# A hybrid encoder layer: the front in another order, keys loaded ahead, W steps and gathers placed elsewhere

## The chip, the cores and the metric

The kernel runs on one core of a Trainium2 chip. The metric is device time in microseconds of one execution. TensorE (PE in the rows) multiplies, VectorE (DVE), ScalarE (ACT) and GpSimd (POOL) do the rest; SyncE (SP), ScalarE and GpSimd issue the transfers.

## The reference

One layer over 528 tokens (16 meta tokens and 512 of the sequence) of width 1024, cut to what matters:

```python
xn = rmsnorm(h, ln1_w)
dq, dk, dv, gq, gk, gv, gr, zf, zb = split(xn @ w_in)
da = rmsnorm(diff_attention(rope(dq), rope(dk), dv, lam, pos), da_subln_w) * (1 - lam_init)   # 4 heads
go = rmsnorm(gla_bidirectional(gq, gk, gv, log_g_f, log_g_b), gla_norm_w) * silu(gr)          # 4 heads
h = (h + concat(da, go) @ w_out)[16:]
# product keys: 8 heads, 2 x 128 keys, 16 of each, 16 of the 256 sums; 128 experts a token
q = rmsnorm(h, ln2_w) @ w_q                       # 512 x (8, 2, 128)
ts, ti = top_k(q @ sub_keys, 16)                  # per head and half
best, pos = top_k(ts[0][:, None] + ts[1], 16)     # idx of 16384 experts, gate = softmax(best)
out = h + sum_k (gate * gelu(hn . u[idx])) * v[idx]
return rmsnorm(out, final_norm_w)
```

## The kernel before, in words

Every product in float32 is made of three: both operands are split into a `hi` and a `lo` half (`hi` cast by ScalarE at L118, `lo = raw - hi` by VectorE or POOL at L120), and L131 to L133 multiply hi by hi, lo by hi and hi by lo.

The **front** (0 to about 365 us) follows the string `ORDER`, a letter a step: `G` and `g` draw the next part of the two generators of GLA (one for each pair of heads), `x` is the projections of the second pair, `v`, `k` and `q` the projections of attention (`q` ends with a rotation of the positions and a product with the meta keys at L471), `u` one of 16 attention units (L490, L491 the scores, L515, L516 transposes, L522 the values), `w` one of eight output products over the GLA half. The weights are streamed in the order of the same string. At the end of a GLA head its output is transposed at L769.

Then come the second half of the output products, the second norm (L893 its sums, L903 its factors as a row by a product of `ones` and the diagonal tile `dg`), 16 **query products** and behind each the scores against the keys (L953). VectorE picks 16 of 128 per token, head and half (`top16`, L188 to L192), then 16 of the sums (`topk2`, L196 to L255: candidates, positions, expert numbers and the softmax, whose result is written to `sel` at L255); L992 computes the expert numbers `idx` of the first 128 tokens.

The experts are used in two ways. For 384 of the 512 tokens all 16384 experts are computed densely, in 128 **u tiles** (24 matmuls of 128 x 384 each, gelu at L1094) and 128 **v tiles**, weighted by a matrix W that TensorE builds from one-hot vectors: 48 **W steps** of 8 tokens, each with transposes of `sel` first where a new 128 tokens begin (L1002), one-hot operands `oh` from VectorE (L1024, L1029), 32 small matmuls (L1060, L1063) and an evacuation (L1065). The dense results of the first `LA` = 60 u tiles are spilled to memory and so is W, and come back with the v tiles. For the other 128 tokens rows of u and v are **gathered** by indirect DMAs that POOL issues (L264), 128 of each; VectorE dots the u rows (L278) and adds up the v rows (L276).

The numbers that set the mix: W step n stands behind u tile `A0 + int(n * AR)`, and 10 later from step 14 on, where the last two `topk2` stand between; `GS0` is the u tile from which on gathers are issued, `RA` the gathers per u tile from there on, `RV` those per v tile up to the 60th and `RUV` behind it. `lo` of u tiles 0 to 13 is made on POOL, from 14 on on VectorE (`LP` = 14). Within these anchors a scheduler orders the instructions of every engine; tiles with a common tag share buffers, so that a load waits for the last reader of what lay there.

Of the kernel before, what the change touches and what calls it, by code (L numbers as in the profile page):

```python
# [9 lines left out]
F32 = mybir.dt.float32  # L10
# [14 lines left out]
P = 128  # L25
# [9 lines left out]
PH = 8  # L35
NK = 128
# [6 lines left out]
AHEAD = 2  # L43
LAG = 3
GP = 0
GS0 = 12
C1 = 3.0
WB = 4
WL = 1
# [10 lines left out]
VS = 4  # L60
VR = 5
VG = 6
RA = 0.3
RV = 0.85
RUV = 2.92
LA = 60
NCAND = 80
TCA = {'schedule_with_timeline_sim': True}
ORDER = 'GGGxGGGGGGGkGGggvgqggukugguqugguuukuvgqgukqgwuwuuuwwwuuuww'
ATAG = 'a'  # L70
BTAG = '-p'
BL = 32
# [5 lines left out]
PF = 3, 13, 2  # L78
PG = 33, 49, 1
LP = 14  # L80
A0 = 15
AR = 0.48
AG = 10
AL = 14

# [1 line left out]
def _emit(ctx, tc, I, out):  # L87
    nc = tc.nc
# [48 lines left out]
    def split(hi, lo, src, eng=None):  # L137
        last[0] = nc.scalar.copy(hi, src).ins.name  # L138
        (eng or nc.vector).tensor_sub(lo, src, hi.bitcast(F32))  # L139
# [40 lines left out]
    def tz(name, shape, dt=F32):  # L180
        tag = "t" + TMAP[name]
        return f2.tile(list(shape), dt, name=name, tag=tag, bufs=TBUF[TMAP[name]])

    def fx(name, shape, tag, dt=F32):
        return f1.tile(list(shape), dt, name=name, tag=tag)
# [113 lines left out]
    cnt = dict.fromkeys("vkqgGxuw", 0)  # L299
    for step in ORDER + "w" * (KD - ORDER.count("w")):  # L300
        n = cnt[step]
# [506 lines left out]
    cnt = dict.fromkeys("vkqgGxuw", 0)  # L808
    for step in ORDER:
        n = cnt[step]  # L810
# [59 lines left out]
    def hn_hi(k):  # L870
        return hg[k // 4][0][:, k % 4, :]

    def hn_lo(k):
        return hg[k // 4][1][:, k % 4, :]
# [21 lines left out]
    nc.scalar.copy(hss, hs[:, :NT])  # L896
    rstd(hrs, hss, D)
    nc.vector.scalar_tensor_tensor(hn0, acc0, hrs[:, 0:1], hn0, op0=ALU.mult, op1=ALU.mult)
    dg = tz("dg", [P, 4, P])
    for t in range(NT):  # L900
        nc.vector.tensor_scalar(dg[:, t, :], ident, hrs[:, t:t + 1], None, op0=ALU.mult)
    b = bank(tag=PT["nat"])
# [16 lines left out]
    qs = qst.enter_context(tc.tile_pool(name="qs", bufs=1))  # L919

    iof = w1.tile([P, NK], F32, name="iof")
    nc.sync.dma_start(out=iof, in_=I["iota"].to_broadcast([P, NK]))
    keys = qs.tile([P, 2 * PH, NK], F32, name="keys")
    nc.sync.dma_start(out=keys, in_=I["keys"])

    tsv = tk1.tile([P, 2, NT, 4, 2, TOPK], F32, name="tsv")
    tiv = tk1.tile([P, 2, NT, 4, 2, TOPK], U32, name="tiv")
# [11 lines left out]
    for k in range(KD):  # L939
        hk = qs.tile([P, ND], F32, name="hk", bufs=2)  # L940
        nc.gpsimd.tensor_add(hk, hn_hi(k)[:, P:].bitcast(F32), hn_lo(k)[:, P:].bitcast(F32))
        nc.gpsimd.tensor_mul(hk, hk, hrow[:, P:])
        split(un_hi[:, k, :], un_lo[:, k, :], hk, nc.gpsimd)

    tks = []
    for hp in range(2 * PH):
# [34 lines left out]
    def wbuild():  # L981
        def tgt(n):
            return A0 + int(n * AR) + (AG if n >= AL else 0)

        def fin_all(at):
            while fins:
                fins.pop(0)(at)

        for tk in tks:
            for _ in tk:  # L990
                pass
        nc.vector.scalar_tensor_tensor(idx, sel[:, 1, 0].rearrange("p h r -> p (h r)"), float(NK),  # L992
                                       sel[:, 2, 0].rearrange("p h r -> p (h r)"), op0=ALU.mult, op1=ALU.add)
        yield A0 - 2
        fin_all(A0 - 2)
        cur = {}
# [132 lines left out]
    def pull(n):  # L1129
        credit[0] += n  # L1130
        while credit[0] >= 1.0:
            credit[0] -= 1.0
            next(sp, None)
# [12 lines left out]
    def w_load(b):  # L1146
        if b * WI < NK and b not in WA:
            wa = vp.tile([P, 2, WI, ND], F32, name="wa", bufs=3)
            wt = wa[:, 0].rearrange("p w n -> p (w n)").rearrange("p (b w n) -> p b w n", w=WI, n=BL)
            nc.sync.dma_start(out=wt, in_=W_d[:, :, b * WI:b * WI + WI, :])  # L1150
            if b * WI < LA:
                nc.sync.dma_start(out=wa[:, 1], in_=A_d[:, b * WI:b * WI + WI, :])
            WA[b] = wt, wa[:, 1]
# [5 lines left out]
    for i in range(LA):  # L1159
# [4 lines left out]
        if i == LA - ET:  # L1164
# [5 lines left out]
            w_load(0)  # L1170
        if GS0 <= i < LA - ET - GP:
            pull(RA)

    acts = {}
    for i in range(NK):
# [12 lines left out]
        if i >= VS:  # L1188
            pull(RV if i < LA else RUV)
    for _ in sp:  # L1190
# [112 lines left out]
```

## Time and profile before

| | before |
|---|---|
| median of 3 runs | 1642.83 us (1638.16 to 1642.96) |
| profiled execution | 1635.18 us |
| its span, first to last instruction | 1633.4 us |
| TensorE busy | 1561.7 us (96%) |
| VectorE busy | 1261.5 us (77%) |
| mean granted clock of TensorE | 0.985 |

The rows below are of the one profiled execution; what lies around its span is 1.8 us. A busy share of TensorE contains its stretches at the lower clock.

### The profile page before, as it was taken

The page shows a single profiled execution, that of the slowest core. Times are in us where ns is not written, and L with a number is a line of the kernel's source. Part 1 is how long each engine was busy: PE and PEld are TensorE (multiplying, and loading weights), DVE is VectorE, ACT ScalarE, POOL GpSimd, SP SyncE. Part 2 cuts the span into 40 slices and gives each one's busy share as a digit, 9 for nine tenths or more (in the row PEclk, how much of TensorE's full clock was granted, in tenths as well). Part 3 has the DMA queues.
Part 4 walks back from the last instruction along what each step waited for, and adds up shares of the span by engine and source line. Part 5 has one row for each costly group of instructions (what it writes and reads, how often), then busy time and mean ns, then how long its engine had stood idle before and what let it go on. Part 6 is the DMA issues. An engine that isn't in the chain of part 4 may idle for free.

```text
span 1633.4 us, 24035 instructions
## 1 busy us (share of the span) xinstructions
PE 1561.7 (96%) x8793; PEld 1382.3 (85%) x8793; DVE 1261.5 (77%) x2492; ACT 712.7 (44%) x1131; POOL 563.7 (35%) x419
## 2 busy tenths in 40 slices
PE   6999999999997789999999999999999999999997
PEld 6887886778897788989888888889999999998886
DVE  3888767655999796977467787788878887787877
ACT  5444654544332466777343333333333333333333
POOL 3445113048553330040011112265454443444442
PEclk9999999999999899999999999999999999999999
DMA  7112212233233466778999998799999999999975
GB/s 235 59 48 83 66 55 69 84 104 118 79 133 112 133 235 241 296 265 304 375 350 323 319 315 312 272 369 360 324 348 330 330 338 318 329 353 328 331 252 193
DMA packets 152358, 387.40 MB, mean 237 GB/s; under 512 B 12752, under 2 KB 71376, under 8 KB 150576
## 3 DMA queue, kind: packets, MB, share of 16 engines
q1 hardware_dynamic: 104432, 213.62, 38.0%
q0 software_dynamic: 36864, 134.23, 23.2%
q10 hardware_dynamic: 10944, 38.02, 6.2%
q8 instruction: 69, 1.13, 0.3%
q14 instruction: 49, 0.40, 0.1%
HBM read 342.56 MB, written 40.63 MB: 235 GB/s over the span
## 4 chain that ended last, share of the span: by engine, by line
PE 46%; issue 19%; DVE 15%; DMA 10%; POOL 7%; ACT 2%; SPq 1%; POOLq 0%; ACTq 0%; DVEq 0%
POOL gat L264 7%; PE bankg L131 6%; PE bankg L133 6%; PE bankg L132 6%; PE banka L1119 5%; PE banka L1122 5%; PE banka L1123 5%; DMA gat<-v,idx 4%; DMA gat<-u,idx 3%; PE bankp L1123 2%; PE bankp L1122 2%; PE bankp L1119 2%; DVE tiv L192 1%; DVE tiv L189 1%; DVE sc L190 1%
## 5 line engine op out<-in xcount | busy, mean ns | idle before, releaser
L264 POOL DMA_INDIRECT gat<-u,idx x128 | 201.6, 1575 | 531.2 <-PE bankp L1123 251.6
L118 ACT CAST hi<-raw 128x1024 fp32r<-128x1024 f32 x177 | 185.8, 1051 | 320.3 <-PE bankg L132 191.1
L131 PE MATMUL bankg<-un_hi,hi 128*128 128x384 f32 x896 | 303.4, 339 | 3.9 <-ACT act L1094 3.9
L132 PE MATMUL bankg<-un_lo,hi 128*128 128x384 f32 x896 | 302.5, 338 | 0.0
L133 PE MATMUL bankg<-un_hi,lo 128*128 128x384 f32 x896 | 302.3, 338 | 0.0
L264 POOL DMA_INDIRECT gat<-v,idx x128 | 157.7, 1232 | 206.7 <-PE bankp L1123 172.7
L120 DVE TENSOR_TENSOR lo<-raw,hi 128x1024 fp32r<-128x1024 f32 x142 | 174.0, 1227 | 56.3 <-ACT hi L118 52.4
L276 DVE SCALAR_TENSOR_TENSOR acc<-gat,sact,acc 128x1024 f32<-128x1024 f32 x128 | 164.3, 1284 | 58.1 <-DMA gat<-v,idx 55.0
L278 DVE CUSTOM_DVE_ANT_0 gat<-gat,hn 128x1024 f32<-128x1024 f32 x128 | 155.1, 1219 | 36.8 <-DMA gat<-u,idx 36.1
L139 DVE TENSOR_TENSOR vhl<-vraw,vhl 128x1024 fp32r<-128x1024 f32 x128 | 156.1, 1220 | 27.6 <-ACT vhl L138 26.5
L131 PEld LDWEIGHTS bankg<-un_hi,hi 128*128 128x128 f32 x896 | 169.6, 189 | 7.9 <-ACT act L1094 4.2
L132 PEld LDWEIGHTS bankg<-un_lo,hi 128*128 128x128 f32 x896 | 169.5, 189 | 3.3
L133 PEld LDWEIGHTS bankg<-un_hi,lo 128*128 128x128 f32 x896 | 169.6, 189 | 1.7 <-DVE lo L120 0.2
L138 ACT CAST vhl<-vraw 128x1024 fp32r<-128x1024 f32 x128 | 134.2, 1049 | 55.8 <-PE bankp L1123 34.6
L120 POOL TENSOR_TENSOR lo<-raw,hi 128x1024 fp32r<-128x1024 f32 x35 | 87.1, 2491 | 73.7 <-ACT hi L118 70.1
L1065 ACT ACTIVATE stg<-banka 128x512 f32<-128x512 f32 x96 | 96.9, 1165 | 11.4 <-PE banka L1063 11.0
L1094 ACT ACTIVATE act<-bankg 128x384 f32<-128x384 f32 x112 | 54.5, 487 | 30.2 <-PE bankg L133 20.7
L133 PE MATMUL bankp<-un_hi,lo 128*128 128x384 f32 x128 | 44.6, 348 | 21.9 <-DVE lo L120 21.9
L1024 DVE TENSOR_TENSOR oh<-iT,ioh 128x2048 f16<-128x2048 f16 x48 | 57.5, 1219 | 1.3 <-PE banka L1063 1.3
L1029 DVE TENSOR_TENSOR oh<-oh,gs 128x2048 f16<-128x2048 f16 x48 | 57.7, 1218 | 0.0
L1060 PE MATMUL banka<-oh 128*128 128x128 f16 x384 | 49.5, 221 | 8.2 <-DVE oh L1029 7.3
L1063 PE MATMUL banka<-oh 128*128 128x128 f16 x384 | 49.1, 220 | 0.0
(2287 smaller groups left out, 3775.1 us busy)
## 6 DMA issues: line engine op xcount, KB each, us to landing
raw<-uT SPq DMA_DIRECT2D x128, 512.0 KB
vraw<-v SPq DMA_DIRECT2D x128, 512.0 KB
W_d<-stg ACTq DMA_DIRECT2D x12, 2048.0 KB
wa<-W_d SPq DMA_DIRECT2D x32, 768.0 KB
A_d<-act ACTq DMA_DIRECT2D x60, 192.0 KB
wa<-A_d SPq DMA_DIRECT2D x15, 768.0 KB
raw<-wq SPq DMA_DIRECT2D x16, 512.0 KB
raw<-win_n SPq DMA_DIRECT2D x12, 512.0 KB
```

The costliest lines, as they stand in the source:

```text
L118: nc.scalar.copy(hi, raw)
L120: (eng or nc.vector).tensor_sub(lo, raw, hi.bitcast(F32))
L131: nc.tensor.matmul(o, lhsT=ah, rhs=bh, start=start, stop=False)
L132: nc.tensor.matmul(o, lhsT=ah, rhs=bl, start=False, stop=False)
L133: return nc.tensor.matmul(o, lhsT=al, rhs=bh, start=False, stop=stop)
L138: last[0] = nc.scalar.copy(hi, src).ins.name
L139: (eng or nc.vector).tensor_sub(lo, src, hi.bitcast(F32))
L264: g = nc.gpsimd.indirect_dma_start(out=r, out_offset=None, in_=src, in_offset=bass.IndirectOffsetOnAxis(ap=idx[:, hk:hk + 1], axis=0))
L276: nc.vector.scalar_tensor_tensor(acc0, r, sact[:, hk:hk + 1], acc0, op0=ALU.mult, op1=ALU.add)
L278: nc.vector.tensor_tensor_reduce(r, r, hn0, scale=1.0, scalar=0.0, op0=ALU.mult, op1=ALU.add, accum_out=sact[:, hk:hk + 1])
L1119: m0 = nc.tensor.matmul(o, lhsT=gh_[:, tc_], rhs=vh[:, dc], start=(j == 0), stop=False, skip_group_check=True)
L1122: nc.tensor.matmul(o, lhsT=gh_[:, tc_], rhs=vl[:, dc], start=False, stop=False, skip_group_check=True)
```

## The change

Five numbers and the string are others, the keys' load is issued behind the loop that makes `un_hi`, in the program's order, and the diagonal tile lies in another place:

```diff
-GS0 = 12
+GS0 = 20
...
-RA = 0.3
+RA = 0.15
 RV = 0.85
-RUV = 2.92
+RUV = 3.0
...
-ORDER = 'GGGxGGGGGGGkGGggvgqggukugguqugguuukuvgqgukqgwuwuuuwwwuuuww'
+ORDER = 'GGxGGvGkGGGqGGGGggugkugguqguguvgkuguqgugkuguqwuwuwuwuwuwuww'
...
-A0 = 15
-AR = 0.48
+A0 = 11
+AR = 0.56
...
-    dg = tz("dg", [P, 4, P])
+    dg = fx("dgh", [P, 4, P], "gvs")
...
     iof = w1.tile([P, NK], F32, name="iof")
     nc.sync.dma_start(out=iof, in_=I["iota"].to_broadcast([P, NK]))
-    keys = qs.tile([P, 2 * PH, NK], F32, name="keys")
-    nc.sync.dma_start(out=keys, in_=I["keys"])
...
         split(un_hi[:, k, :], un_lo[:, k, :], hk, nc.gpsimd)
+    keys = qs.tile([P, 2 * PH, NK], F32, name="keys")
+    nc.sync.dma_start(out=keys, in_=I["keys"])
```

The first W steps stand behind u tiles 11 to 18 (before 15 to 21), the others behind 28 to 47 (before 31 to 47).

What that does to the engines' order. SP's queue at the keys, as a piece of the difference (`raw<-wq` are blocks of the query weights, `hT_d` parts of the layer's input written out):

```order
 L112 DMA raw<-wq 128x1024
 L853 DMA hT_d<-hT_3443 128x384
 L853 DMA hT_d<-hT_3460 128x384
 L112 DMA raw<-wq 128x1024
+L943 DMA keys<-keys 128x2048
 L922 DMA iof<-iota 128x128
-L924 DMA keys<-keys 128x2048
 L112 DMA raw<-wq 128x1024 x11
```

The keys stand one row ahead of `iof` instead of behind it.

TensorE at the end of the front, before (`mix` are the output products of a `w` step, `rdst` the rotated queries of head 3, whose product with the meta keys is L471):

```order
L133 MATMUL bankg<-mix_hi_2963,lo 128x512
L131 MATMUL bankg<-mix_hi_2963,hi 128x512
L132 MATMUL bankg<-mix_lo_2965,hi 128x512
L133 MATMUL bankg<-mix_hi_2963,lo 128x512
L132 MATMUL bankg<-mix_lo_2965,hi 128x512
L133 MATMUL bankg<-mix_hi_2963,lo 128x512
L471 MATMUL bankp<-rdst,kb 32x512
L515 MATMUL banka<-ident,pr 128x128 x4
L516 MATMUL banka<-ident,pr 32x128
L769 MATMUL banka<-ident,gy 128x128
L490 MATMUL banka<-stl,stq_2685 128x512
L491 MATMUL banka<-stk_2404,stq_2685 128x512
```

and in the change (`stq_2982` and `stq_2983` are the queries of head 3):

```order
L515 MATMUL bankp<-ident,pr 128x128 x4
L516 MATMUL bankp<-ident,pr 32x128
L490 MATMUL banka<-stl,stq_2982 128x512
L490 MATMUL banka<-stl,stq_2983 128x512
L515 MATMUL banka<-ident,pr 128x128 x4
L516 MATMUL banka<-ident,pr 32x128
L522 MATMUL bankp<-vN_494,aT 128x128
L522 MATMUL bankp<-vN_495,aT 128x128
L522 MATMUL bankp<-vN_496,aT 128x128
L522 MATMUL bankp<-vN_497,aT 128x128
L522 MATMUL bankp<-vN_498,aTm 128x128
L471 MATMUL bankp<-rdst,kb 32x512
```

L471 of head 3 stood right behind an output product and ahead of the last GLA head's transposes. It now stands behind attention units of head 2, behind the first two score products of head 3, and behind all of L769.

TensorE at the first score product L953, before (the query products of the weights' columns, `hg` being the normed input):

```order
L132 MATMUL banka<-hg_lo_3504,hi 128x512
L133 MATMUL banka<-hg_hi_3503,lo 128x512
L131 MATMUL banka<-hg_hi_3647,hi 128x512
L132 MATMUL banka<-hg_lo_3648,hi 128x512
L133 MATMUL banka<-hg_hi_3647,lo 128x512
L131 MATMUL banka<-hg_hi_3647,hi 128x512
L953 MATMUL bankg<-keys,pq 128x128 x4
L132 MATMUL banka<-hg_lo_3648,hi 128x512
```

and in the change, from L903 on, with the row ahead of it:

```order
L133 MATMUL bankg<-hg_hi_3647,lo 128x512
L903 MATMUL banka<-dgh,ones 128x512
L131 MATMUL banka<-hg_hi_3503,hi 128x512
L132 MATMUL banka<-hg_lo_3504,hi 128x512
L131 MATMUL banka<-hg_hi_3503,hi 128x512
L132 MATMUL banka<-hg_lo_3504,hi 128x512
L953 MATMUL bankg<-keys,pq 128x128 x4
L133 MATMUL banka<-hg_hi_3503,lo 128x512
```

Before, 40 query matmuls stand between L903 and the first L953, in the change 4. The number of query matmuls behind L903 is the same, 312.

VectorE where the top-k of the first 256 tokens ends, before, from the expert numbers L992 to the second write of the gates (L255):

```order
L992 SCALAR_TENSOR_TENSOR idx<-sel 128x128
L220 TENSOR_SCALAR sm_row<-sm_bp 128x128
L221 TENSOR_SCALAR sm_bp<-sm_bp 128x128
L226 CAST sm_rf<-sm_row 128x128
L227 CAST sm_cf<-sm_bp 128x128
L229 SCALAR_TENSOR_TENSOR sm_t_6141<-sm_rf,sm_cf 128x128
L120 TENSOR_TENSOR lo<-raw,hi 128x1024 x3
L253 TENSOR_REDUCE zs<-sm_gate 128x8 x2
L254 RECIPROCAL zs<-zs 128x8 x2
L255 TENSOR_TENSOR sel<-sm_gate,zs 128x2x64 x2
L210 TENSOR_TENSOR sm_gate<-sm_bsv 128x128
L278 ISA gat,sact<-gat,hn_70 128x1024
```

and in the change, from the last write of the gates on:

```order
L255 TENSOR_TENSOR sel<-sm_gate,zs 128x2x64
L220 TENSOR_SCALAR sm_row<-sm_bp 128x128
L210 TENSOR_TENSOR sm_gate<-sm_bsv 128x128
L247 TENSOR_TENSOR sel<-eq 128x2x64
L210 TENSOR_TENSOR sm_gate<-sm_bsv 128x128
L221 TENSOR_SCALAR sm_bp<-sm_bp 128x128
L226 CAST sm_rf<-sm_row 128x128
L212 TENSOR_TENSOR sm_gate<-sm_gate,hrs 128x128
L239 TENSOR_TENSOR eq<-sm_cb,io16b 128x2048
L212 TENSOR_TENSOR sm_gate<-sm_gate,hrs 128x128
L227 CAST sm_cf<-sm_bp 128x128
L120 TENSOR_TENSOR lo<-raw,hi 128x1024
```

The gates' two writes are no longer behind three `lo` of u tiles but in among the last steps of the top-k: ahead of the second one stand L239, L243, three rows of L245 and L253 to L255 that were behind `idx`. The first `lo` that VectorE makes (u tile 14's) stands 11 rows behind it. On TensorE, the transposes of `sel` (L1002) stand behind 308 matmuls of u tiles, before behind 384, and the first matmul of a W step behind 399, before 473; the 14 tiles whose `lo` POOL makes are 336.

## Rows read from the trace of the kernel before

**Rows 1.** The page: the span, and the busy us, share of the span and instructions of each engine.

```profile
span 1633.4 us, 24035 instructions
...
PE 1561.7 (96%) x8793; PEld 1382.3 (85%) x8793; DVE 1261.5 (77%) x2492; ACT 712.7 (44%) x1131; POOL 563.7 (35%) x419
```

**Rows 2.** The waits of TensorE over the whole span: line and operand waited for, us in total, times, longest.

```profile
PE bankp L133 <- DVE lo L120: 21.9, 2, 19.7
...
PE banka L1060 <- DVE oh L1029: 7.3, 5, 3.4
...
PE bankg L131 <- ACT act L1094: 3.9, 1, 3.9
PE bankg L582 <- POOL hi L577: 3.2, 1, 3.2
```

**Rows 3.** Stretches of 30 us: length, then busy us and instructions of each engine, the granted clock of TensorE, the share of DMA and its GB/s.

```profile
270.00:300.00 30.00, 26.00 (x95) 16.60 (x93) 21.05 (x53) 15.59 (x50) 4.14 (x3) 0.77 0.20 56
510.00:540.00 30.00, 10.25 (x59) 9.93 (x58) 29.93 (x174) 2.87 (x4) 1.46 (x2) 0.75 0.09 31
570.00:600.00 30.00, 24.86 (x192) 23.64 (x189) 28.35 (x33) 17.33 (x21) 1.48 (x2) 0.94 0.57 202
600.00:630.00 30.00, 26.59 (x207) 25.45 (x206) 25.90 (x27) 18.68 (x23) 13.78 (x2) 0.94 0.75 278
1500.00:1530.00 30.00, 29.34 (x148) 26.29 (x148) 23.91 (x25) 10.23 (x14) 11.51 (x11) 1.00 0.92 335
```

**Rows 4.** The timeline of TensorE at the end of the front: start, us, engine, line, operation, output and inputs, shapes, count, and in brackets the idle time before it with what ended it.

```profile
260.43 0.40 PE L133 MATMUL bankg<-act_hi,lo 128*128 128x512 f32 x1
...
273.02 1.02 PE L471 MATMUL bankp<-rdst,kb 128*32 128x512 f32 x2 [1.98 <-DVE ss L144]
...
276.79 0.30 PE L769 MATMUL banka<-ident,gy 128*128 128x128 f32 x1 [1.89 <-DVE gy L765]
...
290.34 0.63 PE L132 MATMUL bankg<-mix_lo,hi 128*128 128x512 f32 x1
...
292.87 0.39 PE L132 MATMUL bankg<-mix_lo,hi 128*128 128x512 f32 x1
293.10 0.39 PE L133 MATMUL bankg<-mix_hi,lo 128*128 128x512 f32 x1
```

**Rows 5.** The timeline where the query products begin, of TensorE, SyncE's DMA queue (SPq) and VectorE.

```profile
364.62 0.95 PE L893 MATMUL banka<-ones,sq 128*128 128x1 f32 x8
...
373.04 1.02 PE L903 MATMUL banka<-dg,ones 128*128 128x512 f32 x2
...
374.13 0.33 SPq L922 DMA_DIRECT2D iof<-iota  x1
374.55 0.38 SPq L924 DMA_DIRECT2D keys<-keys  x1
...
383.01 1.05 PE L953 MATMUL bankg<-keys,pq 128*128 128x128 f32 x8
...
385.84 0.87 DVE L188 MAX8 tsv<-sc 128x8 f32<-128x128 f32 x4 [16.78 <-issue]
...
393.29 0.88 DVE L188 MAX8 tsv<-sc 128x8 f32<-128x128 f32 x4 [2.67 <-ACT sc L955]
```

**Rows 6.** The timeline of VectorE and TensorE around the long wait.

```profile
519.39 0.34 PE L132 MATMUL bankp<-un_lo,hi 128*128 128x384 f32 x1
...
520.31 1.21 DVE L243 TENSOR_TENSOR eq<-eq,tf 128x2048 bf16<-128x2048 bf16 x1
...
536.96 0.27 DVE L992 SCALAR_TENSOR_TENSOR idx<-sel 128x128 int32<-128x128 f32 x1
...
539.47 0.69 PE L133 MATMUL bankp<-un_hi,lo 128*128 128x384 f32 x1 [19.75 <-DVE lo L120]
...
548.04 0.49 DVE L255 TENSOR_TENSOR sel<-sm_gate,zs 128x128 f32<-128x128 f32 x2
```

**Rows 7.** The timeline of POOL, VectorE and TensorE from 555 to 620 us.

```profile
555.22 12.05 POOL L264 DMA_INDIRECT gat<-u,idx  x1 [15.91 <-PE bankg L133]
...
570.39 1.23 DVE L278 CUSTOM_DVE_ANT_0 gat<-gat,hn 128x1024 f32<-128x1024 f32 x1 [3.94 <-DMA gat<-u,idx]
...
573.95 0.44 PE L133 MATMUL bankp<-un_hi,lo 128*128 128x384 f32 x1 [2.16 <-DVE lo L120]
...
585.38 0.44 PE L131 MATMUL bankp<-un_hi,hi 128*128 128x384 f32 x1 [2.98 <-ACT hi L118]
...
616.13 1.23 DVE L278 CUSTOM_DVE_ANT_0 gat<-gat,hn 128x1024 f32<-128x1024 f32 x1 [4.10 <-DMA gat<-u,idx]
...
619.69 0.23 PE L1060 MATMUL banka<-oh 128*128 128x128 f16 x1 [3.41 <-DVE oh L1029]
```

**Rows 8.** The page's costliest groups: line, engine, operation, output and inputs, count, then busy us, mean ns of one, and the idle time before them with what ended most of it.

```profile
L264 POOL DMA_INDIRECT gat<-u,idx x128 | 201.6, 1575 | 531.2 <-PE bankp L1123 251.6
...
L1024 DVE TENSOR_TENSOR oh<-iT,ioh 128x2048 f16<-128x2048 f16 x48 | 57.5, 1219 | 1.3 <-PE banka L1063 1.3
```

**Rows 9.** The timeline of POOL and TensorE at the end.

```profile
1605.16 0.94 POOL L264 DMA_INDIRECT gat<-v,idx  x1 [0.30 <-issue]
1606.40 1.05 POOL L264 DMA_INDIRECT gat<-v,idx  x1 [0.30 <-issue]
...
1625.44 0.39 PE L1123 MATMUL bankp<-vhl,gl__15068 128*128 128x512 f32 x1
```

## The prediction

> **What bounds the kernel now.** I read the busy shares first [rows 1]: TensorE works 1561.7 of 1633.4 us and VectorE 77%, so only what stops TensorE or slows its clock moves the end, and there are 71.7 us without a matmul. The waits of TensorE [rows 2] say on what: 21.9 on `lo` of u tiles, one wait alone 19.7; 7.3 on `oh`, the one-hot operands of the W steps; 3.9 on `act` at the change to the v tiles; and waits of 3.2 or less in the front. The stretches of 30 us [rows 3] add what waits don't show: the granted clock is 0.77 in 270 to 300, 0.75 around the long wait and 0.94 in the two stretches from 570 to 630, while VectorE is full (29.93 of 30) ahead of 540. Late in the v tiles TensorE has 29.34 of 30 us with DMA at 0.92. So three places matter: the end of the front, the hole at 520 to 540 with what follows until 630, and the last microseconds.
>
> **The front's last part.** In the kernel before, the query gemm of head 3 ends near 260.7, its product with the meta keys (L471) starts at 273.02 after a wait of 1.98, and the last GLA head's transposes (L769) then wait 1.89 at 276.79 [rows 4]. The same output product that takes 0.39 at 292.87 takes 0.63 at 290.34: half clock, 1.2 instead of 2.4 GHz. At a mean of 0.77 over 30 us this costs at most (1 - 0.77) x 30 = 6.9 [rows 3]. So the place holds 3.9 us of waits and up to 6.9 of slow clock. In the order of the change the GLA step is drawn ahead of query gemm 3, its transposes stand amid attention and output products, and L471 comes later: between the gemm and the first product that needs its rope stand 24 output products, at 0.23 each by their spacing at 292.87 [rows 4] 5.5 us, and 12 score products and some 30 small products, which I estimate at another 8: 13.5. The chain took 273.02 - 260.7 = 12.3. Both waits should go: -3.9. Whether the clock then stays up I can't read; I take half, -3: **-7**, bounds -10.8 (all of it) and +6 (a stretch of the new front waits for its gates or its rope and falls to half clock as this one did). The earlier part of the front keeps its work and gets projections between the GLA levels instead of behind them; I put it at 0.
>
> A rule of the Trainium skill speaks against counting on this ("TensorE: Matmul & The Clock Gate", section HAM oscillation): the slow clock is the default state, and a stretch in which TensorE idles enough throws it back, once for each such stretch. The trace agrees in that the clock is low at the short waits of the front as well as at the hole [rows 3]. By the rule each wait of the new order may bring a slow stretch of its own, the front's term is -3.9 instead of -7, and the sum below 3 us higher.
>
> **Keys.** Before, the load of `keys` stands behind `iof` on SP's queue; `iof` is issued at 374.13, when L903 (373.04) has freed the buffer it needs, and `keys` follows at 374.55. The first score product L953 starts at 383.01 and the first top-k operation at 385.84, after VectorE had idled 16.78 [rows 5]. In the change `keys` stands ahead of `iof` and waits only for L893 (364.62, 0.95 long): issue at about 365.6, 9 earlier. It took 383.01 - 374.55 = 8.5 to be used, so 374.1 is the earliest; TensorE's order has L953 four matmuls behind L903, 373.04 + 0.9 + 4 x 0.23 = 374.9. The top-k starts 385.84 - 383.01 = 2.8 later, as before: 377.7, **8.1 earlier**. Not all of it arrives: a head-part costs VectorE 393.29 - 2.67 - 385.84 = 4.8 us, and now 17 to 30 query matmuls (4 to 7 us) stand between score groups, so it starves until second-level work is at hand. Before it starved 2.67 there; I take 4 (2.7 to 7).
>
> **The hole.** The top-k work up to `idx` (L992, 536.96) is 536.96 - 385.84 - 2.67 = 148.4 us [rows 5, 6]. In the change it ends at 377.7 + 148.4 + 4 = 530.1. Ahead of the second gate write (L255), on which the transposes L1002 wait, now also stand L239 and L243 (1.21 each [rows 6], both on 128x2048), three L245 on half, a quarter and an eighth of that (about 1.2) and L253 to L255 (about 1.3, the last pair being 0.49): 5. So `sel` is there at 535.5. TensorE comes to L1002 28 matmuls sooner than it came to the missing `lo` (539.47 - 19.75 = 519.7); a u matmul of 384 columns, priced from the 512 columns of [rows 4], is 0.23 x 384 / 512 = 0.17: 519.7 - 4.8 = 514.9. Hole 20.6 instead of 19.75: the 28 matmuls given up eat what the keys bring. **+1**, bounds -4 (top-k fed without a gap) and +8 (first rival). The half clock behind the hole stays.
>
> **Behind the hole.** From 555 to 620 TensorE waits 2.16 for a `lo`, 2.98 for a `hi` and 3.41 for an `oh` [rows 7], and the clock's 0.94 in two stretches costs (1 - 0.94) x 60 = 3.6 [rows 3]: 12 us. The first and the third stand behind 3.94 and 4.10 in which VectorE sat before a gathered row (L278); the gather's issue on POOL ahead of the first had taken 12.05 us, against a mean of 1.575 [rows 7, 8]. With gathers from u tile 20 on and half as many per tile, VectorE's order has its first L278 behind the W steps of the first batch: no such wait, and four dots of 1.23 fewer. Against it the 14 W steps of that batch (two VectorE operations of 1.22 each [rows 8]) begin some 75 matmuls (13 us of TensorE) sooner among the u tiles, and the `lo` of tiles 14 and 15 stand behind parts of the last top-k: tile 15's comes, by its place in VectorE's order, about 13 us behind L255, when TensorE wants it after 9.4, a new wait of 3.5. 12 - 3.5 - 2 for its clock gives **-6**, bounds -11 and +3 (VectorE, not the gathers, was the limit, and the waits return with 3.5 more). In the second batch both orders ask for about as much VectorE work per TensorE work: 0. Nor is a change seen at the 3.9 us before the v tiles: 0.
>
> **Late gathers and the tail.** At 0.15 per u tile instead of 0.3, 4.5 instead of 11.4 gathers are done by u tile 49; the rest catches up at 3.0 instead of 2.92 per tile, and three instead of two fall into the last slot. POOL is busy 11.51 of 30 us late in the v tiles [rows 3], so the added ones are hidden; the last is not. Gathers at the end come 1606.40 - 1605.16 = 1.24 apart, 19 us ahead of the last matmul at 1625.44 [rows 9], to which their sums lead through the last weights. One more costs 1.24 and what its DMA adds: **+1.5**, bounds 0 and +4. More gather bytes per tile (2.7% of them) at a DMA share of 0.92 I put at 0, since TensorE hardly waits there.
>
> **Sum.** -7 + 1 - 6 + 1.5 = -10.5. The profiled execution took 1635.18 with its span of 1633.4; the span would be 1622.9, that execution 1624.7. It lies 7.65 below the median of the runs shown (1642.83), so on their scale 1632.3: **1632 us**. A measurement of this kernel can tell about 0.3% (4.9 us) from no change.
>
> **Rivals.**
> - *The transposes wait longer* (slower). If the keys' lead is lost (the load lands late, or VectorE starves by all of it), `sel` comes at 537.2 + 5 + 0.5 = 542.7, and TensorE stands at 514.9: a hole of 27.8, +8. VectorE then is as late as before for the batch, so the -6 goes; with -3.9 in the front and +1.5 at the end +5.6: 1648. It decides where the top-k starts after 381 instead of 377.7. Against it: SP's order frees the load from L903. Chance 0.12.
> - *The new front falls to half clock itself* (the rule above): front +6, sum +2.5, 1645. For it speaks that waits of 2 us went with a slow stretch [rows 3, 4], against it the 13.5 to 12.3 at the place known. Chance 0.15, half of it within 0.3%.
> - *Only the keys and the gathers act*: the front gives 0 and the stalls half, -0.5: 1642, no change. Chance 0.12.
> - *The late gathers bound the end*: POOL falls behind by five gathers of 1.24, +6 at the tail: sum -6, 1637. Chance 0.06.
> - *Everything goes*: hole -4, stalls -11, front -10.8, tail +1.5: -24, 1619. Chance 0.08.
> - The forecast, -5 to -18 (1625 to 1638): 0.47.
>
> Faster: the forecast, everything, and half of the fourth, 0.58. Within 0.3%: the third, half of the second, half of the fourth and a little of the first: 0.24. Slower: the rest, 0.18. The range leaves out the worst hole and the deepest gain: 1617 to 1646; the forecast's own is 1625 to 1638.
>
> **What would show it.** `keys` issued about 365.6 and the first top-k operation about 378; one hole of 19 to 22 us, released by `sel` at L1002 and no longer by `lo`; no VectorE wait on a gathered row before 620; a wait of some 3 us on the `lo` of the next tiles; no waits at L471 and L769 in the front and a clock of 0.9 or more in 260 to 300; three gathers in the last slot. The prediction is wrong if the front shows a new slow stretch, if L1002 waits more than 24, or if `oh` waits grow past 8.

## The result and the profile after

| | before | change |
|---|---|---|
| median of 4 runs each | 1640.86 us (1638.16 to 1642.96) | 1659.26 us (1657.55 to 1660.74) |
| ratio, 95% interval | | 1.0113 [1.0095, 1.0132] |
| span of the profiled execution | 1633.4 us | 1658.7 us |
| mean granted clock of TensorE | 0.985 | 0.969 |

The change is 1.1% slower, where 0.6% faster was forecast. The busy shares of the changed kernel, from its page, beside [rows 1]:

```profile
span 1658.7 us, 24025 instructions
...
PE 1573.5 (95%) x8793; PEld 1391.2 (84%) x8793; DVE 1263.4 (76%) x2492; ACT 716.5 (43%) x1131; POOL 533.8 (32%) x419
```

As many matmuls as before are busy 11.8 us longer, and the time without one grew from 71.7 to 85.2. The loss is in the front. Stretches from the start to where the second norm begins (L893), first of the kernel before, then of the changed one (columns as in [rows 3]):

```profile
0.00:364.60 364.60, 340.91 (x2109) 281.12 (x2110) 255.89 (x573) 188.96 (x418) 114.07 (x112) 0.98 0.28 90
```

```profile
0.00:398.90 398.90, 356.64 (x2111) 291.58 (x2111) 254.09 (x573) 190.88 (x418) 106.11 (x112) 0.92 0.26 82
```

The front is 34.3 us longer: 18.6 of it without a matmul (23.7 to 42.3), 15.7 in the same matmuls running longer, at a clock of 0.92. From L893 to the end the changed kernel takes 1259.8 instead of 1268.8, 9 less. (The two profiled executions differ by 25.3 and the medians by 18.4: that of before lies 6 below its median.)

The waits of TensorE in the changed kernel over the whole span, beside [rows 2]:

```profile
PE bankp L1002 <- DVE sel L255: 24.5, 1, 24.5
PE banka L769 <- DVE gy L765: 9.0, 2, 8.9
...
PE bankg L131 <- ACT act L1094: 5.2, 1, 5.2
PE banka L710 <- DVE ef L706: 3.6, 1, 3.6
...
PE banka L1119 <- ACT gh__15064 L138: 2.7, 1, 2.7
```

The hole is released by `sel` now. New are 8.9 at the transposes L769 and 3.6 at L710 (transposes for the GLA's state); 2.7 at L1119, a product of the v tiles at the very end, was 1.1. Where they lie and what the clock does, in stretches of 30 us:

```profile
120.00:150.00 30.00, 18.01 (x67) 11.43 (x66) 22.32 (x60) 12.13 (x24) 8.74 (x8) 0.69 0.13 39
150.00:180.00 30.00, 27.64 (x175) 23.70 (x176) 14.86 (x39) 11.90 (x27) 8.21 (x8) 0.85 0.12 32
...
270.00:300.00 30.00, 29.04 (x104) 20.49 (x102) 14.88 (x50) 9.98 (x31) 5.34 (x5) 0.69 0.06 13
300.00:330.00 30.00, 25.52 (x107) 16.03 (x106) 22.36 (x64) 18.38 (x50) 4.17 (x3) 0.89 0.23 64
...
600.00:630.00 30.00, 29.93 (x255) 28.67 (x254) 28.69 (x29) 21.83 (x26) 0.00 (x0) 1.00 0.68 253
```

The front has two slow places, 120 to 180 and 260 to 330; behind the hole TensorE is full again soon. The first place in TensorE's timeline (L471 is the first `q`'s product with the meta keys, L619 makes the gates' logits):

```profile
122.33 1.04 PE L471 MATMUL bankp<-rdst,kb 128*32 128x512 f32 x2 [1.54 <-DVE rdst L407]
...
137.59 0.48 PE L754 MATMUL banka<-S,qx 64*128 64x128 f32 x2
137.92 0.29 PE L619 MATMUL bankp<-zT,w 64*128 64x16 f32 x2
147.06 0.45 PE L769 MATMUL banka<-ident,gy 128*128 128x128 f32 x1 [8.86 <-DVE gy L765]
...
147.87 0.79 PE L753 MATMUL banka<-S,qx 64*128 64x128 f32 x2
```

and in VectorE's, in the gap (L641 and L672 belong to the gates of the next pair of heads, L144 to L147 and L765 to the norm of the pair that is done):

```profile
139.83 1.37 DVE L641 TENSOR_TENSOR_SCAN pre<-ones,garr 128x129 f32<-128x129 f32 x4
...
141.91 0.16 DVE L144 TENSOR_SCALAR ss<-ss 128x4 f32<-128x4 f32 x1
...
143.81 0.74 DVE L641 TENSOR_TENSOR_SCAN pre<-ones,garr 128x129 f32<-128x129 f32 x2
...
146.58 1.13 DVE L765 SCALAR_TENSOR_TENSOR gy<-go,rs,gr 128x128 f32<-128x128 f32 x4
```

The norm's small steps go in turn with the next pair's gates, and TensorE's next instruction is the one that needs their end. The query projection (`q`) that could stand there was drawn four GLA steps earlier. Behind the gap the GLA products run at the slow clock: two of L753 take 0.79, where two of L754, of the same shape, took 0.48 ahead of it. The gap is not the only slow stretch there. The clock in stretches of 3 us (columns as above):

```profile
126.00:129.00 3.00, 3.00 (x7) 2.00 (x7) 2.15 (x6) 0.00 (x0) 0.21 (x1) 0.50 0.46 115
...
135.00:138.00 3.00, 3.00 (x20) 2.34 (x18) 0.38 (x2) 0.00 (x0) 0.00 (x0) 1.00 0.00 0
...
150.00:153.00 3.00, 3.00 (x11) 2.33 (x12) 0.83 (x3) 0.00 (x0) 0.00 (x0) 0.50 0.00 0
```

Half clock (1.2 GHz) comes first behind the waits of 1.5 at L471, the end of the early `q`, and 0.8 right after it, until about 131, and again from the gap to about 159.

### The profile page after: what moved, and what is told of

The parts are those of the page before. It is cut to its first block, busy times and chain, and to the rows that moved or that the text cites. A ratio compares the mean times of both kernels' runs of the same rounds, so it can differ in the third digit from the quotient of the medians.

```text
span 1658.7 us, 24025 instructions
## 1 busy us (share of the span) xinstructions
PE 1573.5 (95%) x8793; PEld 1391.2 (84%) x8793; DVE 1263.4 (76%) x2492; ACT 716.5 (43%) x1131; POOL 533.8 (32%) x419
## 4 chain that ended last, share of the span: by engine, by line
PE 66%; DVE 15%; DMA 6%; issue 6%; ACT 4%; POOL 3%; SPq 1%; ACTq 0%; POOLq 0%; DVEq 0%
PE bankg L131 9%; PE bankg L132 9%; PE bankg L133 9%; PE banka L1122 7%; PE banka L1119 7%; PE banka L1123 7%; PE bankp L1119 3%; PE bankp L1122 3%; PE bankp L1123 3%; DMA raw<-uT 1%; DVE oh L1024 1%; POOL lo L120 1%; DVE lo L120 1%; PE banka L656 1%; ACT stg L1065 1%
## 5 line engine op out<-in xcount | busy, mean ns | idle before, releaser
L264 POOL DMA_INDIRECT gat<-u,idx x128 | 169.6, 1325 | 566.9 <-PE bankp L1123 238.0
L264 POOL DMA_INDIRECT gat<-v,idx x128 | 169.2, 1322 | 181.3 <-PE bankp L1123 153.8
L1060 PE MATMUL banka<-oh 128*128 128x128 f16 x384 | 48.5, 220 | 3.0 <-DVE oh L1029 2.1
L131 PE MATMUL bankg<-act_hi,hi 128*128 128x264 f32 (+1 forms) x144 | 48.6, 337 | 1.9 <-ACT rraw L400 1.9
L131 PE MATMUL bankg<-hi,act_hi 128*128 128x256 f32 x160 | 46.4, 290 | 2.1 <-ACT vN L777 1.4
```

The costliest lines, as they stand in the source:

```text
L131: nc.tensor.matmul(o, lhsT=ah, rhs=bh, start=start, stop=False)
L264: g = nc.gpsimd.indirect_dma_start(out=r, out_offset=None, in_=src, in_offset=bass.IndirectOffsetOnAxis(ap=idx[:, hk:hk + 1], axis=0))
```

## The experiments

The theory under test first: the loss is the query projection drawn too early, which leaves TensorE nothing behind the first pair's norm, and the slow clock that follows the wait. Against it: the loss comes only with the other edits, or it lies in the later part of the order, at the place of `v` or elsewhere.

All are timed against the kernel before. "Rest" is the span less the start of L893, from the profiled execution. Kernels with the front of before (e2, e5 to e9) start L893 at 359.3 to 367.4, so one profile tells some 4 us either way there. The profiled executions lie between 6 us below and 10 us above the medians of their kernels (e1 10 above, e8 9, e12 and e14 5).

| kernel | ratio [95%] | L893 at | rest |
|---|---|---|---|
| before | 1 | 364.6 | 1268.8 |
| change | 1.0113 [1.0095, 1.0132] | 398.9 | 1259.8 |
| e1, order only | 1.0179 [1.0146, 1.0213] | 397.2 | 1281.2 |
| e2, all but the order | 0.9919 [0.9886, 0.9952] | 367.2 | 1261.5 |
| e3, change with `q` later | 1.0014 [0.9992, 1.0036] | 376.4 | 1261.5 |
| e12, e3 with `v` later | 1.0019 [0.9993, 1.0045] | 387.6 | 1260.1 |
| e4, first third of the order | 1.0086 [1.0061, 1.0111] | 376.5 | 1271.2 |
| e14, e4 with `q` later | 1.0030 [1.0002, 1.0059] | 371.5 | 1278.4 |
| e13, later part of the order | 1.0040 [1.0014, 1.0066] | 366.0 | 1273.9 |
| e10, two letters exchanged | 0.9965 [0.9940, 0.9989] | 361.9 | 1270.3 |
| e7, keys | 0.9972 [0.9950, 0.9995] | 363.4 | 1270.5 |
| e5, gathers | 0.9940 [0.9922, 0.9959] | 364.4 | 1258.1 |
| e6, W steps | 1.0086 [1.0053, 1.0120] | 359.3 | 1284.3 |
| e8, keys and W steps | 1.0031 [1.0001, 1.0061] | 364.9 | 1285.9 |
| e9, keys and gathers | 0.9897 [0.9858, 0.9935] | 367.4 | 1258.0 |
| e11, e9 and the exchange | 0.9876 [0.9843, 0.9910] | 361.5 | 1258.7 |
| e15, e11 with a faster catch-up | 0.9861 [0.9819, 0.9902] | 362.5 | 1253.7 |

### Is it the order? The order alone, and all the rest alone

e1 is the kernel before with the new string:

```diff
-ORDER = 'GGGxGGGGGGGkGGggvgqggukugguqugguuukuvgqgukqgwuwuuuwwwuuuww'
+ORDER = 'GGxGGvGkGGGqGGGGggugkugguqguguvgkuguqgugkuguqwuwuwuwuwuwuww'
```

> The kernel before with the new order string alone; keys, W steps and gathers as before. Theory A (the order of the front makes the whole loss): the column sums L893 come about 34 us later than in the kernel before (364.6), with the wait of about 9 at L769 near 147 and half clock behind it and again around 265 to 290; the hole and the rest keep their length, so the run is 28 to 36 us longer (ratio 1.017 to 1.022). Theory B (the loss comes from keys, the diagonal tile's new place or the weights' transfers colliding with them): under 5 us longer.

e2 is the change with the string of before:

```diff
-ORDER = 'GGxGGvGkGGGqGGGGggugkugguqguguvgkuguqgugkuguqwuwuwuwuwuwuww'
+ORDER = 'GGGxGGGGGGGkGGggvgqggukugguqugguuukuvgqgukqgwuwuuuwwwuuuww'
```

> The change with the old order string: keys ahead of iof, W steps from u tile 11, gathers from u tile 20 stay. Theory A: L893 within 1 us of the kernel before, and the run 6 to 10 us shorter than it (ratio 0.994 to 0.996), as the change made up 8.6 us between the first u tile and the v tiles. Theory B: as long as the kernel before or longer.

Measured: the order alone costs 1.79%, all the rest together wins 0.81%, somewhat more than forecast. The waits of e1:

```profile
PE bankp L133 <- DVE lo L120: 22.9, 3, 19.7
PE banka L769 <- DVE gy L765: 9.0, 2, 8.9
```

The hole of before and the new front's wait stand side by side, so the front's loss comes from the string and not from the keys or the gathers. e2's hole is that of the change, 24.5 on `sel`, with the front of before.

### Is it the place of `q`? The first third, and `q` two steps later

e3 is the change with one letter moved:

```diff
-ORDER = 'GGxGGvGkGGGqGGGGggugkugguqguguvgkuguqgugkuguqwuwuwuwuwuwuww'
+ORDER = 'GGxGGvGkGGGGGqGGggugkugguqguguvgkuguqgugkuguqwuwuwuwuwuwuww'
```

> The change with one letter moved in its order: the first query projection stands ahead of the last two GLA steps of pair 0 instead of ahead of the last four. Theory A1 (TensorE waits at L769 because no projection is left to cover the norm of the GLA heads): the wait of 8.9 shrinks below 3, the clock in 120 to 150 rises from 0.69 to above 0.9, and the run is 8 to 15 us shorter than the change. Theory A2 (the GLA chain on VectorE and ScalarE is the bound of this stretch whatever TensorE has to do): the wait turns up at another product of the chain, and less than 4 us are won.

e4 is before with the new string's first 16 letters:

```diff
-ORDER = 'GGGxGGGGGGGkGGggvgqggukugguqugguuukuvgqgukqgwuwuuuwwwuuuww'
+ORDER = 'GGxGGvGkGGGqGGGGgggggukugguqugguuukuvgqgukqgwuwuuuwwwuuuww'
```

> The kernel before with the first 21 steps (up to the first attention unit) in the manner of the change: same projections and GLA steps, but the value, key and query projections drawn early, so that the last GLA steps stand alone; everything behind the first attention unit as before. Theory A1: most of the loss is here, the first attention unit comes 15 to 20 us later and the run is 15 to 20 longer (ratio 1.009 to 1.013). Theory A3 (the loss lies in the later half of the front, in the GLA steps between attention units): under 6 us longer.

e14 is e4 with `q` moved as in e3:

```diff
-ORDER = 'GGxGGvGkGGGqGGGGgggggukugguqugguuukuvgqgukqgwuwuuuwwwuuuww'
+ORDER = 'GGxGGvGkGGGGGqGGgggggukugguqugguuukuvgqgukqgwuwuuuwwwuuuww'
```

> The kernel before with the new first third in which the query projection is moved two GLA steps later, and the old order behind the first attention unit. The same first third without that move gave 1.0086, with the wait of 10 at L769. If the letter cures the first third: the wait below 3, L893 within 3 us of 364.6, ratio 0.998 to 1.002. If what is left of the loss sits in the first third: L893 8 or more later, ratio above 1.004.

Measured: e4 loses 0.86%, 14 us, just under the forecast. TensorE's waits in it from 100 to 180 us, the longest:

```profile
PE banka L769 <- DVE gy L765: 10.0, 1, 10.0
```

In e3 no wait from 100 to 180 is longer than 1.6, and its two stretches there are:

```profile
120.00:150.00 30.00, 27.64 (x148) 21.01 (x147) 23.29 (x71) 16.11 (x34) 10.90 (x10) 0.89 0.18 51
150.00:180.00 30.00, 29.48 (x237) 26.88 (x236) 19.72 (x38) 14.71 (x34) 8.82 (x11) 1.00 0.20 62
```

148 and 237 matmuls in place of 67 and 175, at clocks of 0.89 and 1.00 instead of 0.69 and 0.85. One letter two places on takes back 0.99% of the time of before, 16 us. In e14 the same letter takes back 0.56%, 9 of e4's 14 us; the 0.30% that e14 still loses fits neither of its two forecasts, and its cause stays open. So the early `q` is shown as the cause at the first place. That is about half of the order's loss: with the other edits the order costs 1.94% (the change against e2), and e3 still stands 0.95% above e2. The string also sets the order of the weights; what released L769 was VectorE, at a DMA share of 0.13, so it was not a load that TensorE waited for. How much of the 16 us is the wait and how much the slow clock was not measured apart; in e3 a wait of 1.6 is left near 137, with a shorter slow stretch behind it.

### The second place: `v` later, and the later part alone

e12 is e3 with the value projection behind two more attention units:

```diff
-ORDER = 'GGxGGvGkGGGGGqGGggugkugguqguguvgkuguqgugkuguqwuwuwuwuwuwuww'
+ORDER = 'GGxGGvGkGGGGGqGGggugkugguqgugugkuguvqgugkuguqwuwuwuwuwuwuww'
```

> The change with two letters moved: the first query projection two GLA steps later (which won back 1.0% of its own), and the second value projection, which nothing needs before the ninth attention unit, from ahead of GLA step 8 of pair 1 to behind its step 9. Theory A1 (projections must be left for the stretches in which a GLA step hangs on VectorE): the wait of 3.6 at L710 goes, the clock of 240 to 270 rises from 0.77 to above 0.9, L893 comes 6 to 10 sooner than with the first letter alone (376.4), ratio 0.995 to 0.998 against the kernel before. Theory A2 (it is the chain's own length): L893 within 2 us of 376.4, ratio 1.000 to 1.002.

Measured: no faster than e3. The wait moved to no other place, it grew from 3.6 in e3:

```profile
PE banka L710 <- DVE ef L706: 5.5, 1, 5.5
```

and the clock in 240 to 270 is no better than e3's 0.77:

```profile
240.00:270.00 30.00, 23.04 (x90) 16.21 (x89) 15.85 (x49) 10.93 (x31) 2.54 (x2) 0.72 0.10 29
```

The theory that `v` is missing there falls. What L710 waits for, the trace of the change tells. ScalarE, VectorE and TensorE at this place:

```profile
259.29 1.26 ACT L412 CAST stq<-rdst 64x512 fp32r<-64x512 f32 x2 [3.65 <-DVE rdst L407]
...
262.52 0.62 ACT L699 ACTIVATE ef<-pre 128x512 f32<-128x512 f32 x1
```

```profile
262.65 0.50 DVE L505 SCALAR_TENSOR_TENSOR zt<-zz 128x2 f32<-128x2 f32 x1 [2.01 <-ACT pr L502]
...
263.52 0.69 DVE L706 TENSOR_TENSOR ef<-ef,gk 128x512 f32<-128x512 f32 x1
```

```profile
264.36 0.89 PE L710 MATMUL banka<-ident,ef 128*128 128x128 f32 x4 [3.61 <-DVE ef L706]
```

L706 needs L699, whose input `pre` was complete at about 145. In ScalarE's order L699 stands behind the cast of rotated queries, which waited 3.65 for VectorE, and behind the softmax of an attention unit; VectorE in turn waits 2.01 for that softmax at L505, ahead of L706. The rows of e1 and e3 show the same order there. So at the second place TensorE waits for attention work that stands ahead of the GLA step on ScalarE and VectorE, and not for the step's own input. That is read from the traces; no run moved it.

e13 is the front of before up to its first attention units, with the new string's order behind:

```diff
-ORDER = 'GGGxGGGGGGGkGGggvgqggukugguqugguuukuvgqgukqgwuwuuuwwwuuuww'
+ORDER = 'GGGxGGGGGGGkGGggvgqggukuuqguguvgkuguqgugkuguqwuwuwuwuwuwuww'
```

> The kernel before with the new order from the first attention unit on, behind the old first third (the old one has drawn three more GLA steps of pair 1 by then, so the first three between units are left out). Theory J (the later part costs by itself): L893 8 to 15 us later than 364.6, waits at L710 or L769 and half clock between 240 and 330, ratio 1.004 to 1.009. Theory K (its loss only follows from a GLA pair that starts late behind the new first third): L893 within 3 us of 364.6, ratio 0.998 to 1.002.

Measured: 0.40% slower, as the first theory has it, while its profile's L893 stands only 1.4 later than before, as the second has it; the two are not told apart. First third (0.86%) and later part (0.40%) make 1.26%; the order alone costs 1.79%. The difference of some 9 us is hardly larger than the three intervals leave open; if it is real, what makes it stays open.

### Is the end of the front as the forecast has it?

e10 exchanges one GLA step and the last query projection of before, which is the step that my -7 rested on:

```diff
-ORDER = 'GGGxGGGGGGGkGGggvgqggukugguqugguuukuvgqgukqgwuwuuuwwwuuuww'
+ORDER = 'GGGxGGGGGGGkGGggvgqggukugguqugguuukuvgqgukgqwuwuuuwwwuuuww'
```

> The kernel before with two neighbouring letters of its order exchanged: the last GLA step of pair 1 ahead of query projection 3, as in the change. This is the part of the forecast that was to win 7 us in the front. If the forecast's mechanism holds: no waits at L471 and L769 near 275, clock above 0.9 in 270 to 300, 4 to 10 us shorter (ratio 0.994 to 0.9975). Rival: the wait moves to the first product that needs the rotated queries or to the GLA norm, and the clock falls anyway: within 2 us.

Measured: 0.35% faster, 5.7 us. One of the two waits is left, and the stretch that had 0.77 [rows 3] has 0.89:

```profile
PE banka L769 <- DVE gy L765: 1.9, 1, 1.9
```

```profile
270.00:300.00 30.00, 26.69 (x109) 17.42 (x108) 20.26 (x56) 15.92 (x51) 4.89 (x4) 0.89 0.26 73
```

The wait of L471 goes; the transposes still wait. The time is what the forecast asked for. The clock is a weak witness here: the seven profiles with the order of before have 0.66 to 0.94 in this stretch, four of them 0.77, the three with the exchange (e10, e11, e15) 0.89, 0.94 and 0.89.

### The four edits behind the front

e7 has the keys and the diagonal tile of the change alone:

```diff
-    dg = tz("dg", [P, 4, P])
+    dg = fx("dgh", [P, 4, P], "gvs")
...
-    keys = qs.tile([P, 2 * PH, NK], F32, name="keys")
-    nc.sync.dma_start(out=keys, in_=I["keys"])
...
+    keys = qs.tile([P, 2 * PH, NK], F32, name="keys")
+    nc.sync.dma_start(out=keys, in_=I["keys"])
```

> The kernel before with the keys' load and the diagonal tile's place of the change alone; W steps, gathers and order as before. Theory G: the first top-k operation comes 8 to 10 us sooner, starving costs 2 more, idx comes 6 to 7.5 sooner, the hole of 19.7 shrinks to about 13, and all of it reaches the end: 5 to 8 shorter (ratio 0.995 to 0.997). Rival: the lo of the next u tiles or POOL's work beside the top-k eats it: under 2 shorter.

Measured: 0.28% faster, 4.6 us, between the two forecasts; the hole shrinks from 19.7 to 17.5 only, where 13 was expected.

e5 has the gathers alone:

```diff
-GS0 = 12
+GS0 = 20
...
-RA = 0.3
+RA = 0.15
...
-RUV = 2.92
+RUV = 3.0
```

> The kernel before with the gathers' three numbers alone (from u tile 20, 0.15 per u tile, 3.0 per late v tile). Theory C (the waits behind the hole come from VectorE sitting before gathered rows): the waits of VectorE of 3.9 and 4.1 before L278 ahead of 620 go, TensorE's waits on lo and oh behind the hole fall by 4 to 6 and the v tiles start 3 to 6 earlier; at the end TensorE waits 1 to 3 longer for the last act: the run is 1 to 5 shorter (ratio 0.997 to 0.9995). Theory D (VectorE's amount of work is the limit there, gathers or not): the v tiles start within 1 us, the run is 1 to 3 longer.

Measured: 0.60% faster, more than the 1 to 5 us expected, although the hole grows to 24.0. VectorE's waits for gathered rows from 540 to 640, before and in e5:

```profile
DVE gat L278 <- DMA gat<-u,idx: 8.0, 2, 4.1
```

```profile
DVE gat L278 <- DMA gat<-u,idx: 2.3, 1, 2.3
```

e6 has the W steps alone, e8 the W steps with the keys of e7:

```diff
-A0 = 15
-AR = 0.48
+A0 = 11
+AR = 0.56
```

> The kernel before with the W steps' two numbers alone (from u tile 11, 0.56 per step). The transposes L1002 stand behind 295 u matmuls instead of 384. Theory E (TensorE then waits for the gates sooner, and top-k ends no sooner): the hole grows from 19.7 to 25 to 29 and starts about 7 us sooner; of that, the W steps done inside what were stalls give back some, the run is 0 to 6 longer. Theory F (W steps sooner are worth more than the longer hole, since VectorE then works on one-hot operands while TensorE stands): the run is 2 to 8 shorter.

> Keys, diagonal tile and W steps of the change, gathers and order as before. If the parts add up: the sum of what keys alone and W steps alone gave, within 2 us. If keys pay only with the sooner W steps (or the other way round): 4 or more apart from the sum. The hole stands at the transposes L1002 and is 20 to 25 us long.

e9 is the change without them and with the order of before:

```diff
-A0 = 11
-AR = 0.56
+A0 = 15
+AR = 0.48
...
-ORDER = 'GGxGGvGkGGGqGGGGggugkugguqguguvgkuguqgugkuguqwuwuwuwuwuwuww'
+ORDER = 'GGGxGGGGGGGkGGggvgqggukugguqugguuukuvgqgukqgwuwuuuwwwuuuww'
```

> Keys, diagonal tile and gathers of the change; old order string and old W steps. Gathers alone gave 0.9940, keys alone 0.9972, all but the order 0.9919. Theory H (the sooner W steps cost in any case, as they did alone, 1.0086): 0.9915 by the sum of the two parts or lower, with no wait at L1002 and a hole on lo of 17 to 22. Theory I (sooner W steps pay once the gathers are out of their way): above 0.9925, that is slower than all but the order.

Measured: W steps sooner cost 0.86% by themselves, 14 us where at most 6 were expected. The waits of e6:

```profile
PE bankp L1002 <- DVE sel L255: 25.9, 1, 25.9
PE banka L1119 <- ACT gh__8339 L138: 10.0, 1, 10.0
```

A hole of 25.9, and a wait of 10.0 at the first v tiles. Together with the keys (e8) they are still 0.31% slower than before, some 4 us less than the two parts add up to, which the intervals don't tell apart. With keys and late gathers it is 0.9919 with them (e2) and 0.9897 without (e9), again inside the intervals. With late gathers the rest is 1253.7 to 1261.5 in all eight kernels that have them, with early ones 1268.8 to 1285.9 in all nine others; they stay apart when each execution's distance from its median is taken off. The gathers alone part the two groups.

### The tail, and a version that beats both

e11 is e9 with the exchange of e10 (its only difference from e9):

```diff
-ORDER = 'GGGxGGGGGGGkGGggvgqggukugguqugguuukuvgqgukqgwuwuuuwwwuuuww'
+ORDER = 'GGGxGGGGGGGkGGggvgqggukugguqugguuukuvgqgukgqwuwuuuwwwuuuww'
```

> The two before together: keys, diagonal tile, gathers and the exchanged letters. If all parts add up: 0.986 to 0.990. If the exchange gives nothing: as keys and gathers without it, about 0.9915.

e15 is e11 with the gathers of the v tiles caught up sooner, so that the last is issued ahead of the last slot:

```diff
-RUV = 3.0
+RUV = 3.06
```

> Keys, gathers and the exchanged letters (0.9876), with 3.06 instead of 3.0 gathers per late v tile, so that the last gather is issued ahead of the last slot. If the third gather in the last slot makes the wait for the last weights (3.6 there, 1.1 in the kernel before): that wait falls to 0.5 to 2 and the run is 1 to 3 shorter (ratio 0.986 to 0.9875). Otherwise the wait stays at 3 or more.

The wait of the last v products for their sums, in e11 and in e15:

```profile
PE banka L1119 <- ACT gh__15064 L138: 3.6, 1, 3.6
```

```profile
PE banka L1119 <- ACT gh__15079 L138: 0.3, 1, 0.3
```

Measured: 0.9876 and 0.9861. What the exchange adds to e9 (0.9897) is inside the intervals. The wait at the end goes with the third gather in the last slot; 3.3 is its price in these two profiles, and the kernels with three gathers there wait 2.7 to 4.7. The difference in time, 2.5 us, is inside the intervals too. e15 is the fastest version that ran: 1617.96 us, 1.4% below before and 2.5% below the change.

## Why the prediction was wrong, point by point

**The step that failed** is the sentence "The earlier part of the front keeps its work and gets projections between the GLA levels instead of behind them; I put it at 0". It keeps its work, but I looked only at where projections go and not at what they leave: the place behind the last GLA step of the first pair, where TensorE needs independent work while VectorE does the norm. In place of the 0 the order alone cost 1.79% (e1), and one early `q` made about half of that (e3, 16 us); the other half lies in the later places and was not taken apart. In the profile that part cost 8.9 at L769, 3.6 at L710 and slow clock around both, 34.3 us in all with the end of the front. The bound of +6 that I gave the front was made from the one slow place of before, a wait of 2 [rows 4]; behind its first load that front holds no wait above 3.2. What the order of TensorE did show is that no gemm stands ahead of L769 any more.

**The end of the front (-7).** The two waits that I priced at -3.9 are gone in the change:

```profile
309.60 0.30 PE L769 MATMUL banka<-ident,gy 128*128 128x128 f32 x1 [0.15 <-DVE gy L765]
...
324.78 1.04 PE L471 MATMUL bankp<-rdst,kb 128*32 128x512 f32 x2
```

Whether the clock's -3 came with them can't be told: three other waits of 0.7 and a slow stretch from about 316 to 322 lie between these rows. e10, the exchange alone, gave -5.7, near the -7, but by another share: there the transposes still wait 1.9.

**The rival with a chance of 0.15**, a slow stretch in the new front, is what happened, at five to six times its price. The Trainium skill ("TensorE: Matmul & The Clock Gate", section HAM oscillation) has an idle stretch throw the engine back to the slow clock, each time anew; the trace agrees, with 0.50 behind the 8.9 us wait and 0.69 in 270 to 300, behind the 3.6 us wait at L710, each a slow stretch of its own.

**Keys.** Predicted: issue 1.0 behind L893 and the first top-k operation 13.1 behind. The changed kernel's rows, SyncE's queue, TensorE and VectorE:

```profile
398.87 0.95 PE L893 MATMUL banka<-ones,sq 128*128 128x1 f32 x8
...
399.88 0.33 SPq L943 DMA_DIRECT2D keys<-keys  x1
...
410.85 0.87 DVE L188 MAX8 tsv<-sc 128x8 f32<-128x128 f32 x4 [6.39 <-issue]
```

1.0 and 12.0; before it was 21.2, so the start is 9.2 earlier for 8.1 forecast. VectorE starves 4.6 later on, forecast 4.

**The hole (+1).** 24.47, forecast 20.6, just over my own mark of 24:

```profile
571.19 0.26 DVE L992 SCALAR_TENSOR_TENSOR idx<-sel 128x128 int32<-128x128 f32 x1
```

```profile
572.11 0.90 PE L1002 MATMUL bankp<-ident,sel 128*128 128x128 f32 x3 [24.47 <-DVE sel L255]
```

`idx` comes 172.3 behind L893, as before: the 9.2 are used up. 1.9 went to starving and about 5 to the moved operations, which I had behind `idx`. The rest, some 2.3, I had not counted: single operations of the top-k take longer, some of them beside a `lo` of POOL. Before, that fell on others, so the 2.3 is a difference of two sums that were not taken apart. L227 and L221 before, then L227 in the change (shortest, median and longest of four, in ns):

```profile
L227 DVE CAST sm_cf<-sm_bp x4: 209/217/220, 451.7 to 537.7; 128x128 f32<-128x128 uint32 x4
```

```profile
L221 DVE TENSOR_SCALAR sm_bp<-sm_bp x4: 214/222/2031, 447.6 to 537.4; 128x128 uint32<-128x128 uint32 x4
```

```profile
L227 DVE CAST sm_cf<-sm_bp x4: 208/212/2200, 475.2 to 574.5; 128x128 f32<-128x128 uint32 x4
```

TensorE came to L1002 148.8 behind L893 for 150.3 forecast, `sel` came 2.4 later than forecast. The two make the 3.9. A bound of +8 held it.

**Behind the hole (-6).** Right in sign, too small in size. In the changed kernel VectorE waits for no gathered row before 640, and the waits on `oh` are 2.1 for 7.3 [rows 2]; the clock is back at 1.00 in 600 to 630 (0.94 before). The -6 had a new wait of 3.5 on a `lo` in it that did not come. The change's rest is 9.0 shorter with a hole 4.7, a start of the v tiles 1.3 and a tail 1.6 longer, so by difference some -17 came behind the hole, past my bound of -11. Of it 10.4 are waits on `oh`, `lo` and `hi` behind the hole (12.5 before, 2.1 now); of the other 6 about 4 are matmuls that ran shorter (TensorE is busy 1216.9 from L893 on, before 1220.7). By e5 the gathers alone give about -10 with a hole 4.3 longer.

**Tail (+1.5).** L1119 waits 2.7 at the end, 1.1 before: +1.6, inside the bounds, and e15 speaks for the third gather as its cause. **The v tiles' start**, put at 0, waits 5.2 instead of 3.9.

So the terms behind the front came out at -9.0 where their sum said -3.5, and the front at +34.3 in the profile (some 29 by the time of e1) where it said -7.

## What to carry to other kernels

A projection that depends on nothing is what hides the next dependent chain: before one is drawn earlier, look at which instruction of TensorE then stands alone behind each norm, and price the norm with what else its engine does in turn. A wait amid small matmuls can cost more than itself: here the 60 us around one of 8.9 and one of 1.5 were granted clocks of 0.69 and 0.85. And a change of five parts is worth trying part by part: the order lost 1.8%, the rest of the change won 0.8%, of which the gathers 0.6%.

## What the runs showed of the hardware

A small VectorE operation can take ten times its time beside a POOL operation: the 128x128 cast at L227 took 2.20 us instead of 0.21 in the change, by the timelines of VectorE and POOL:

```profile
475.25 2.20 DVE L227 CAST sm_cf<-sm_bp 128x128 f32<-128x128 uint32 x1
```

```profile
474.97 2.40 POOL L120 TENSOR_TENSOR lo<-raw,hi 128x1024 fp32r<-128x1024 f32 x1 [5.07 <-ACT hi L118]
```

The cast ends at 477.45 and the `lo` at 477.37. The Trainium skill ("SBUF — State Buffer", section Who interferes with whom) has VectorE and GpSimd share ports as a lock that one holds while the other waits; that the one ends with the other agrees. On POOL's side, the gather's issue of 12.05 among one-hot operations [rows 7] is gone in the change: its longest u gather takes 6.56, and its median is 1.18. What makes an issue long no run shows.

What stays open: what the second slow place (L710, 260 to 330) costs, since no run took its wait away; what e14 still loses in the front; and whether first third and later part cost more together than apart.
